# Two-layer hybrid mLSTM and retention trunk on one core: gate bias on VectorE, new product rows begun tile by tile, layer 1's gate transposes a step later

## The chip, the cores and the metric

The kernel runs on one core of a Trainium2 chip. The metric is the device time of one execution in microseconds (us); lower is better. The time before is the median of three runs, 2317.24 us (2315.03 to 2318.58).

## The reference

Everything is in fp32. The sequence has 1024 tokens, the model is 1024 wide, and there are two layers:

```python
c_act = jax.nn.silu(c)
for l in range(DEPTH):
    ada = c_act @ w_ada[l] + b_ada[l]
    shift, scale, gate = jnp.split(ada, 3, axis=-1)
    h = rmsnorm(x, norm_g[l]) * (1.0 + scale[:, None, :]) + shift[:, None, :]
    p = h @ w_in[l]
    ...
    cell = mlstm_chunkwise(mq_c, mk_c, mv, mi + b_igate[l], mf + b_fgate[l])
    y_m = jax.nn.sigmoid(mo) * head_layernorm(cell, gn_m[l], N_HEADS_MLSTM) * jax.nn.silu(mz)
    ret = retention_chunkwise(rq_h, rk_h, rv)
    y_r = head_layernorm(ret, gn_r[l], N_HEADS_RET) * jax.nn.silu(rz)
    y = jnp.concatenate([y_m, y_r], axis=-1) @ w_out[l]
    x = x + gate[:, None, :] * y
return rmsnorm(x, final_g)
```

Four mLSTM heads and four retention heads are 256 wide each. The change touches three places of this: the vector `gate` (the last third of `ada`), the input and forget gates `mi`, `mf` of the mLSTM heads, and the product with `w_out`.

## The kernel before

**Products.** Each fp32 operand is split into a high part in the fp32r format and a low rest, and a product is made of three fp32r matmuls: high by high, low by high and high by low (`mm3`, lines 133 to 136 of the profile's numbering: L134, L135, L136). ScalarE makes the high part (a cast, L600 or L1005), GpSimd (L601) or VectorE (L1013) subtracts it from the operand. The names `wH`, `wL` are the two parts of a weight tile; parts of activations come from the common pool `b`.

**Order.** The order of TensorE's instructions is written out by hand: the program's order is TensorE's order. For the other engines and for the DMA queue (all loads and stores are issued from SyncE's queue, `SP`), a scheduler orders instructions by its own estimate of time, except in the beginning, and on VectorE and ScalarE from the second product row of an output projection on (`ordered`), where the program's order holds. Each engine runs its instructions in order and waits on semaphores.

Side work is written as Python generators that are started with `launch` and resumed by `tick`. `run_units` calls `tick` after each unit of the main work; `yield n` asks to be resumed n ticks later. So the place of side work among TensorE's instructions is counted in units. A unit is usually 12 matmuls of 512 columns.

**The gate vector** (`gate_rows`, L281 to L293) is such a generator. It is launched after head group 5 of each layer. For each half of 512 columns, VectorE sums eight weight tiles, each scaled by the conditioning vector, into `accs[0]` (128 partitions). A matmul with a matrix of ones (L289) sums over the partitions and puts the result on all 128 of them, in a PSUM tile `pt`. A second matmul (L290) adds the bias: its operands are one row of ones and one row `brow`, which a DMA has loaded from `b_ada` (L286). These two have plain fp32 operands. VectorE copies `pt` into `g` (L292). `g` is used in the output projection.

**The mLSTM gates** (`gate_chain`) run once in each layer, as side work beside the first projections. Scans over the sequence give, for each half of it, a tile `T4` with four groups of four rows (the last of them copied at L484). After `yield 3` TensorE transposes the two `T4` (L494, eight transposes of 128 by 128) and VectorE copies the result into `COL` (L495), from which decays and scales are made.

**The output projection** (`out_projection`, `out_units`) makes the product with `w_out` by seven rows of products in the manner of Strassen-Winograd. Each row has eight items (an activation tile `yH`, `yL` and a weight tile) and four PSUM banks, one for each tile of 128 tokens. A class `OutPrep` loads and splits the items, three ahead of the row. An item is 12 matmuls, three on each of the four banks; behind each item stands a `yield`. The last two items of a row are taken tile by tile: three matmuls of the one and three of the other on a bank, then that bank's read-out. Rows with `first=True` begin on new banks: `b1` (pool `pp`, p = 1), `b2` (pool `pa`, p = 5) and `b3` (pool `pp`, p = 7). The pool `pp` has four banks that are given out in turn; before `b1` the projections use them. The last of these is a half of the z projection of head group 7, which ScalarE reads through a tanh (L528) and VectorE through a product (L530, in `z_evac`).

While the first row runs, the attention of head group 7 is still under way as side work: `scores` (products L134 to L136 and L752 into a bank of `pa`; L754 to L757 on VectorE, then the split `sH`, `sL`), `values` and `update`.

Of the kernel before, what the change touches and what calls it, by code (L numbers as in the profile page):

```python
# [15 lines left out]
ALU = mybir.AluOpType  # L16
# [3 lines left out]
P = 128  # L20

D = 1024
# [4 lines left out]
KT = D // P  # L27
# [42 lines left out]
def tile_hybrid_trunk(ctx, tc, x, c, positions, w_ada, b_ada, norm_g, w_in, conv_w, conv_b,  # L70
                      b_igate, b_fgate, gn_m, gn_r, w_out, final_g, consts, out):
    nc = tc.nc
    V, A, G, PE, Q = nc.vector, nc.scalar, nc.gpsimd, nc.tensor, nc.sync
# [17 lines left out]
    def bt(dt=F32, n=512):  # L91
        return big.tile([P, n], dt, tag="b", name=nm("b"))

    def wt(tag, n, bufs, dt=F32):
        return wrk.tile([P, n], dt, tag=tag, bufs=bufs, name=nm(tag))

    def ps_a():
        return pa.tile([P, 512], F32, tag="a", name=nm("pa"))
# [34 lines left out]
    def mm3(o, lt, rt, start, stop, more=False):  # L133
        PE.matmul(o, lt[0], rt[0], start=start, stop=False, skip_group_check=more)  # L134
        PE.matmul(o, lt[0], rt[1], start=False, stop=False, skip_group_check=more)  # L135
        PE.matmul(o, lt[1], rt[0], start=False, stop=stop, skip_group_check=more)  # L136
# [3 lines left out]
    ones = cst.tile([P, P], F32, tag="ones", name="ones")  # L140
# [110 lines left out]
    def ada_rows(l, c0, accs):  # L251
        acc = bt()
        accs.append(acc)
        prev = None
        for k in range(KT + 1):
            raw = None
            if k < KT:
                raw = bt()
                Q.dma_start(raw, w_ada[l, k * P:(k + 1) * P, c0:c0 + 512])
            if k == 1:  # L260
                V.tensor_scalar(acc, prev, cact[:, 0:1], None, ALU.mult)
            elif k > 1:
                V.scalar_tensor_tensor(acc, prev, cact[:, k - 1:k], acc, ALU.mult, ALU.add)
            prev = raw
            yield 2
# [15 lines left out]
    def gate_rows(l, res):  # L281
        for half in range(2):
            accs = []
            yield from ada_rows(l, 2 * D + half * 512, accs)
            brow = wt("th", 512, 5)
            Q.dma_start(brow[0:1, :], b_ada[l, 2 * D + half * 512:2 * D + (half + 1) * 512].unsqueeze(0))  # L286
            yield 2
            pt = ps_a()
            PE.matmul(pt, ones, accs[0], start=True, stop=False)  # L289
            PE.matmul(pt, ones[0:1, :], brow[0:1, :], start=False, stop=True)  # L290
            g = bt()
            V.tensor_copy(g, pt)  # L292
            res.append(g)  # L293

    def norm_scale(xt, sst, act_rows=()):
# [141 lines left out]
    def gate_chain(l, pgs, gt):  # L437
# [21 lines left out]
        for half in range(2):  # L459
# [26 lines left out]
            prev = {"bq": bq[0:4, 511:512], "br": br[0:4, 511:512], "mx": mx[0:4, 511:512]}  # L486
            T4s.append(T4)
            yield 1
        yield 3
        for half in range(2):  # L490
            T4 = T4s[half]
            pt = ps_a()
# [535 lines left out]
    def out_units(prep, banks, first, last, evac, deep=2):  # L1028
        def product(i, piece, tt):
            (yH, yL), w = piece  # L1030
            ts = slice(tt * P, (tt + 1) * P)
            mm3(banks[tt], (yH[:, ts], yL[:, ts]), w, first and i == 0, i == KT - 1, not first)

        for i in range(KT - deep):
            piece = prep.take()
            for tt in range(4):
                product(i, piece, tt)
            yield
        pieces = [prep.take() for _ in range(deep)]
        for tt in range(4):  # L1040
            for i in range(deep):
                product(KT - deep + i, pieces[i], tt)
            evac(tt)
            if deep > 2 or tt % 2:
                yield
# [36 lines left out]
    def out_projection(l, prep, gb, fg, nhT):  # L1082
# [10 lines left out]
        x12, x22, x21 = [None] * 4, [None] * 4, [None] * 4  # L1093
        b1 = [ps_p() for _ in range(4)]
        run_units(out_units(prep, b1, True, False, save(b1, c1, None)))
        for step in (prep.sum_up, prep.sum_up, prep.cast):
            step()
        ordered = tc.manual_schedule(engines={mybir.EngineType.DVE, mybir.EngineType.Activation})
        ordered.__enter__()
        x11 = [residual(l, 0, 0, tt) for tt in range(4)]  # L1100
        run_units(out_units(prep, b1, False, True,
                            lambda tt: out_rows(l, 0, 0, tt, b1[tt], gb, xn[0], ss[0], x11[tt])))
        b2 = [ps_a() for _ in range(4)]
        run_units(out_units(prep, b2, True, False, save(b2, c5, 0)))

        def sum_up(tt):
# [133 lines left out]
    accs = [bt()]  # L1240
# [7 lines left out]
    for l in range(DEPTH):  # L1248
# [14 lines left out]
        if l == 0:  # L1263
# [6 lines left out]
            for step in script.split():  # L1270
# [6 lines left out]
                elif what == "C":  # L1277
                    half, k = seq[n]
                    hT[k][half] = (bt(F32R), bt(F32R))
                    A.copy(hT[k][half][0], hfs[n])  # L1280
                elif what == "U":
                    half, k = seq[n]
# [3 lines left out]
                elif what == "A":  # L1286
                    g, a, b = (int(d) for d in arg)
# [34 lines left out]
        vraw = []  # L1322
        run_units(v0_units(l, load_v0(l) if l else w0, hT, vraw, pgs))
        launch(gate_chain(l, pgs, gt), 1)
        if l == 0:
            wz1 = split_w(rz1[0], P) + split_w(rz1[1], P)
# [7 lines left out]
        for hg in range(8):  # L1334
# [33 lines left out]
            if hg == 5:  # L1368
                launch(gate_rows(l, gb))
# [40 lines left out]
```

## Time and profile before

| | |
|---|---|
| median of three runs | 2317.24 us (2315.03 to 2318.58) |
| the profiled execution: its own time | 2319.17 us |
| its span, first to last instruction | 2317.5 us |
| TensorE busy | 2262.3 us |
| VectorE busy | 1473.7 us |
| ScalarE busy | 955.8 us |
| GpSimd busy | 813.3 us |
| mean granted TensorE clock | 0.993 |

The profile names the engines PE (TensorE's matmuls), PEld (its weight loads), DVE (VectorE), ACT (ScalarE), POOL (GpSimd) and SP (SyncE's DMA queue). A row of a timeline has the start in us from the span's start, the duration in us, the engine, the line of the kernel, the operation, the tiles (written tile, arrow, read tiles), the number of instructions merged in it, and in brackets the engine's idle time before it with what ended it. A row of the view of waits has who waited for whom, the total in us, the number of waits and the longest. A busy PE may still run at half its clock, so starts of successive matmuls tell more than their durations.

### The profile page before, as it was taken

How to read it: one execution, taken by the hardware profiler on the slowest of the kernel's cores; microseconds unless marked ns; L12 is line 12 of the kernel's file. 1: busy time of each engine (PE TensorE's matmuls, PEld its weight loads, DVE VectorE, ACT ScalarE, POOL GpSimd, SP SyncE). 2: the span in 40 equal slices, each digit the busy share in tenths (PEclk: the TensorE clock that was granted, in tenths of full speed). 3: DMA queues.
4: the chain of work that ended last, by engine and by line, in shares of the span. 5: the costliest groups of instructions: out<-in, count | busy, mean ns of one | idle time of the engine just before them, and what ended most of it. 6: DMA issues, size and time to landing. Idle time of an engine off the chain costs nothing. (4 is left out here: it accounts for less than half of the span.)

```text
span 2317.5 us, 35197 instructions
## 1 busy us (share of the span) xinstructions
PE 2262.3 (98%) x12405; PEld 1948.0 (84%) x12405; DVE 1473.7 (64%) x2971; ACT 955.8 (41%) x1868; POOL 813.3 (35%) x777
## 2 busy tenths in 40 slices
PE   5999999999999999999999999999999999999998
PEld 4888888889988988888888888888898888888886
DVE  7386668566575657557865765575655565665677
ACT  5535433444433323345344544444443333333533
POOL 0344343334354434320152433444334443442100
PEclk9999999999999999999999999999999999999999
DMA  7234434454675665676622335454545545645764
GB/s 247 70 77 122 121 82 150 113 167 135 187 214 181 206 203 170 196 272 205 236 74 66 80 103 138 129 175 114 186 128 175 161 139 177 199 128 186 278 197 153
DMA packets 385729, 367.52 MB, mean 159 GB/s; under 512 B 82420, under 2 KB 268540, under 8 KB 385552
## 3 DMA queue, kind: packets, MB, share of 16 engines
q1 hardware_dynamic: 385552, 365.28, 51.9%
q8 instruction: 97, 1.59, 0.3%
q14 instruction: 80, 0.66, 0.1%
HBM read 253.99 MB, written 111.18 MB: 158 GB/s over the span
## 5 line engine op out<-in xcount | busy, mean ns | idle before, releaser
L134 PE MATMUL pp<-b,wH 128*128 128x512 f32 x1792 | 712.1, 397 | 1.3 <-ACT b L1280 1.1
L135 PE MATMUL pp<-b,wH 128*128 128x512 f32 x1792 | 708.8, 396 | 1.4 <-DVE b L1283 1.3
L136 PE MATMUL pp<-b,wL 128*128 128x512 f32 x1792 | 708.8, 396 | 0.6 <-POOL wL L601 0.6
L601 POOL TENSOR_TENSOR wL<-raw,wH 128x512 fp32r<-128x512 f32 x274 | 373.3, 1370 | 446.6 <-ACT wH L600 395.6
L136 PEld LDWEIGHTS pp<-b,wL 128*128 128x128 f32 x1792 | 338.6, 189 | 80.1 <-POOL wL L601 1.1
L134 PEld LDWEIGHTS pp<-b,wH 128*128 128x128 f32 x1792 | 339.1, 189 | 73.1 <-issue 1.5
L135 PEld LDWEIGHTS pp<-b,wH 128*128 128x128 f32 x1792 | 338.9, 189 | 73.2 <-DVE b L1283 2.4
L601 POOL TENSOR_TENSOR b<-acc,b 128x256 fp32r<-128x256 f32 (+1 forms) x208 | 210.5, 1028 | 284.4 <-ACT b L600 268.1
L134 PE MATMUL pp<-wH,b 128*128 128x256 f32 (+1 forms) x1024 | 302.8, 296 | 3.6 <-DVE g L530 3.6
L136 PE MATMUL pp<-wH,b 128*128 128x256 f32 (+1 forms) x1024 | 302.6, 295 | 0.0
L135 PE MATMUL pp<-wL,b 128*128 128x256 f32 (+1 forms) x1024 | 302.1, 295 | 0.0
L600 ACT CAST wH<-raw 128x512 fp32r<-128x512 f32 x274 | 167.2, 616 | 155.3 <-PE pp L135 116.2
L134 PEld LDWEIGHTS pp<-wH,b 128*128 128x128 f32 x1024 | 193.2, 189 | 10.2 <-DVE g L530 4.4
L135 PEld LDWEIGHTS pp<-wL,b 128*128 128x128 f32 x1024 | 193.3, 189 | 5.5
L136 PEld LDWEIGHTS pp<-wH,b 128*128 128x128 f32 x1024 | 193.0, 188 | 5.7
L618 DVE SCALAR_TENSOR_TENSOR acc<-pp,cols,acc 128x511 f32<-128x511 f32 (+2 forms) x192 | 142.2, 741 | 17.6 <-ACT acc L613 15.5
L600 ACT CAST b<-acc 128x256 fp32r<-128x256 f32 (+1 forms) x208 | 94.6, 487 | 137.1 <-DVE acc L695 81.1
L134 PE MATMUL pa<-b,b 128*128 128x256 f32 (+2 forms) x384 | 117.3, 305 | 10.1 <-ACT nd L798 8.1
L601 POOL TENSOR_TENSOR sL<-th,sH 128x384 fp32r<-128x384 f32 x64 | 66.6, 1040 | 153.1 <-ACT sH L600 141.2
L136 PE MATMUL pa<-b,b 128*128 128x256 f32 (+2 forms) x384 | 116.5, 303 | 0.0
L135 PE MATMUL pa<-b,b 128*128 128x256 f32 (+2 forms) x384 | 116.3, 303 | 0.0
L601 POOL TENSOR_TENSOR cL<-cf,cH 128x516 fp32r<-128x516 f32 (+1 forms) x48 | 65.3, 1361 | 92.5 <-ACT cH L600 90.3
(288 smaller groups left out, 3887.1 us busy)
## 6 DMA issues: line engine op xcount, KB each, us to landing
raw<-in_w_in_dram SPq DMA_DIRECT2D x274, 256.0 KB
b<-in_w_ada_dram SPq DMA_DIRECT2D x96, 256.0 KB
tsp<-g SPq DMA_DIRECT2D x96, 256.0 KB
b<-tsp SPq DMA_DIRECT2D x96, 256.0 KB
gdr<-g SPq DMA_DIRECT2D x64, 256.0 KB
ndr<-zt SPq DMA_DIRECT2D x128, 128.0 KB
g<-ndr SPq DMA_DIRECT2D x64, 256.0 KB
g<-gdr SPq DMA_DIRECT2D x64, 256.0 KB
```

Of the source, the lines that this page charges most:

```text
L134: PE.matmul(o, lt[0], rt[0], start=start, stop=False, skip_group_check=more)
L135: PE.matmul(o, lt[0], rt[1], start=False, stop=False, skip_group_check=more)
L136: PE.matmul(o, lt[1], rt[0], start=False, stop=stop, skip_group_check=more)
L600: A.copy(dst[0], src)
L601: eng.tensor_tensor(dst[1], src, f(dst[0]), ALU.subtract)
L618: V.scalar_tensor_tensor(acc[:, d:], pt[:, 0:HALF - d], wcol, acc[:, d:], ALU.mult, ALU.add)
```

## The change

Three edits in one. The bias of the gate vector is loaded into all 128 partitions instead of one, the matmul L290 goes, and VectorE adds the bias in the instruction that copied before. In layer 1 `gate_chain` waits four steps instead of three ahead of its transposes. In a row of products on new banks, the first two items are taken tile by tile, with a `yield` behind each second tile.

```diff
@@ gate_rows @@
             brow = wt("th", 512, 5)
-            Q.dma_start(brow[0:1, :], b_ada[l, 2 * D + half * 512:2 * D + (half + 1) * 512].unsqueeze(0))
+            Q.dma_start(brow, b_ada[l, 2 * D + half * 512:2 * D + (half + 1) * 512].unsqueeze(0).to_broadcast([P, 512]))
             yield 2
             pt = ps_a()
-            PE.matmul(pt, ones, accs[0], start=True, stop=False)
-            PE.matmul(pt, ones[0:1, :], brow[0:1, :], start=False, stop=True)
+            PE.matmul(pt, ones, accs[0], start=True, stop=True)
             g = bt()
-            V.tensor_copy(g, pt)
+            V.tensor_tensor(g, pt, brow, ALU.add)
@@ gate_chain @@
-        yield 3
+        yield 4 if l else 3
@@ out_units @@
-        for i in range(KT - deep):
+        done = 0
+        if first:
+            pieces = [prep.take(), prep.take()]
+            for tt in range(4):
+                for i in range(2):
+                    product(i, pieces[i], tt)
+                if tt % 2:
+                    yield
+            done = 2
+        for i in range(done, KT - deep):
             piece = prep.take()
             for tt in range(4):
                 product(i, piece, tt)
```

In the changed kernel all lines from L287 to L1033 have numbers lower by one, and those behind the inserted block higher by eight.

**The gate vector.** On TensorE, in the middle of a projection of head group 6 in layer 0, before (`pa` is the PSUM tile `pt`, the rows around it are the projection's):

```order
L136 MATMUL pp_1771_9667<-b_121_880,wL_1767_9658 128x512
L289 MATMUL pa_1774_9687<-b_1618_8939,ones_77 128x512
L290 MATMUL pa_1774_9687<-th_1759_9628,ones_77 128x512
L134 MATMUL pp_1771_9667<-b_138_945,wH_1769_9663 128x512
L135 MATMUL pp_1771_9667<-b_139_946,wH_1769_9663 128x512
```

The row L290 is gone in the changed kernel, here and at the three other places; nothing around it moves on TensorE. On VectorE, at the same place, the rows now are (L291 is the addition; the two rows below it read the projection's bank `pp`):

```order
L908 TENSOR_TENSOR g_1773_9685<-g_1773_9685,g_1801_9787 128x512
L291 TENSOR_TENSOR b_1775_9689<-pa_1774_9687,th_1759_9628 128x512
L882 TENSOR_TENSOR g_1803_9793<-g_1802_9792,g_1803_9793 128x512
L692 TENSOR_TENSOR th_1778_9706<-pp_1771_9667,nd_1274_7223 128x512
L693 TENSOR_TENSOR th_1779_9707<-pp_1771_9667,dm_1272_7217 128x512
```

The addition stands where the copy stood, and reads the tile `th` of the bias besides.

**The first row of products.** On TensorE, the beginning of the first product row of layer 0 before, with item 0 on the four banks 2122 to 2125, then a step of the attention's scores:

```order
L134 MATMUL pp_2122_11439<-wH_2079_11260,b_2077_11258 128x512
L135 MATMUL pp_2122_11439<-wL_2080_11261,b_2077_11258 128x512
L136 MATMUL pp_2122_11439<-wH_2079_11260,b_2078_11259 128x512
L134 MATMUL pp_2123_11440<-wH_2079_11260,b_2077_11258 128x512
...
L134 MATMUL pp_2125_11442<-wH_2079_11260,b_2077_11258 128x512
L135 MATMUL pp_2125_11442<-wL_2080_11261,b_2077_11258 128x512
L136 MATMUL pp_2125_11442<-wH_2079_11260,b_2078_11259 128x512
L134 MATMUL pa_2135_11473<-b_1914_10421,b_1990_10767 128x256
```

And in the changed kernel, with items 0 and 1 (`wH_2079` and `wH_2083`) on banks 2122 and 2123, then the scores, then bank 2124:

```order
L134 MATMUL pp_2122_11437<-wH_2079_11258,b_2077_11256 128x512
...
L134 MATMUL pp_2122_11437<-wH_2083_11264,b_2081_11262 128x512
...
L136 MATMUL pp_2123_11438<-wH_2083_11264,b_2082_11263 128x512
L134 MATMUL pa_2145_11491<-b_1914_10420,b_1990_10765 128x256
...
L134 MATMUL pp_2124_11439<-wH_2079_11258,b_2077_11256 128x512
L135 MATMUL pp_2124_11439<-wL_2080_11259,b_2077_11256 128x512
```

The fourth bank comes up behind 18 matmuls of the row and the scores, where it came up behind nine matmuls and ahead of the scores. The scores stand behind 12 matmuls as before.

**The transposes of layer 1.** On TensorE before, in the middle of a half of a projection (bank 14040):

```order
L136 MATMUL pp_14040<-b_13267,wL_13990 128x512
L494 MATMUL pa_14053<-ident,b_13785 128x128 x4
L494 MATMUL pa_14059<-ident,b_13904 128x128 x4
L134 MATMUL pp_14040<-b_13278,wH_13995 128x512
L135 MATMUL pp_14040<-b_13279,wH_13995 128x512
```

And in the changed kernel, at the end of that half:

```order
L134 MATMUL pp_14038<-b_13309,wH_13993 128x512
L135 MATMUL pp_14038<-b_13310,wH_13993 128x512
L136 MATMUL pp_14038<-b_13309,wL_13994 128x512
L493 MATMUL pa_14080<-ident,b_13783 128x128 x4
L493 MATMUL pa_14086<-ident,b_13902 128x128 x4
```

The eight transposes moved behind 12 more matmuls.

## The prediction

> **What bounds the kernel now.** First the page's busy times and the granted clock, in tenths, over 40 slices.
>
> ```profile
> PE 2262.3 (98%) x12405; PEld 1948.0 (84%) x12405; DVE 1473.7 (64%) x2971; ACT 955.8 (41%) x1868; POOL 813.3 (35%) x777
> PEclk9999999999999999999999999999999999999999
> ```
>
> TensorE is busy for 98% of the span at nearly full clock; no other engine comes above 64%. So time goes only where TensorE has fewer instructions, or waits less, or runs less at half clock. Next the waits of TensorE by whom they were for (total us, times, longest):
>
> ```profile
> PE pa L134 <- ACT nd L798: 8.1, 4, 4.2
> PE pp L134 <- DVE g L530: 3.6, 2, 1.8
> PE pa L134 <- ACT n L840: 1.9, 2, 1.7
> PE pa L494 <- DVE b L484: 1.2, 1, 1.2
> ```
>
> Two of these rows are touched by the change: the wait for L530 (a product row's fourth bank, one in each layer) and the wait for L484 (the transposes in layer 1). The other two are not. The third part of the change takes instructions away.
>
> **The gate vector.** TensorE in layer 0, around one of the four places:
>
> ```profile
> 858.16 0.40 PE L135 MATMUL pp<-b,wH 128*128 128x512 f32 x1
> 858.40 0.40 PE L136 MATMUL pp<-b,wL 128*128 128x512 f32 x1
> 858.63 1.02 PE L289 MATMUL pa<-b,ones 128*128 128x512 f32 x2
> 859.58 1.12 PE L290 MATMUL pa<-th,ones 1*128 1x512 f32 x2
> 860.63 0.50 PE L134 MATMUL pp<-b,wH 128*128 128x512 f32 x1
> ```
>
> Starts tell the cost, since matmuls overlap. An fp32r matmul takes 858.40 - 858.16 = 0.24 of the queue, and the plain fp32 product L290, although it has one row to multiply, takes 860.63 - 859.58 = 1.05 (two instructions). Four places make **4.2 us** saved. Nothing hides L290: the work behind it is TensorE's own.
>
> What is added: VectorE reads a second operand where it copied, and a DMA brings 256 KB where it brought 2. The copy and its nearest rows, additions or products with a PSUM operand of the same shape:
>
> ```profile
> 862.94 0.68 DVE L292 COPY b<-pa 128x512 f32<-128x512 f32 x1
> L694 DVE TENSOR_TENSOR th<-pp,dm 128x512 f32<-128x512 f32 x32 | 21.8, 680 | 0.0
> ```
>
> They take 0.68 each, so VectorE has the same work. The load is issued far ahead; the nearest row for its duration is the broadcast of one row for the attention's mask, 128 KB:
>
> ```profile
> 842.39 0.36 SPq L286 DMA_DIRECT2D th<-in_b_ada_dram  x1
> 2039.16 0.32 SPq L286 DMA_DIRECT2D th<-in_b_ada_dram  x1
> 2055.70 1.02 PE L289 MATMUL pa<-b,ones 128*128 128x512 f32 x2
> 1358.00 0.43 SPq L733 DMA_DIRECT2D dm<-mdr  x1
> 1362.41 0.42 POOL L735 TENSOR_SCALAR_AFFINE_SELECT dm<-dm 128x256 f32<-128x256 f32 x1 [6.68 <-DMA dm<-mdr]
> ```
>
> That one took 1362.41 - 1358.00 = 4.4. The bias has 862.94 - 842.39 = 20.6 before VectorE reads it, and at the last place at least 2055.70 - 2039.16 = 16.5. Twice 4.4 for twice the bytes, as an upper bound, is 8.8, still within it. I cost it at nothing; what is hidden is the landing, under the projection's matmuls. If the cover were gone, VectorE would stand at the addition, with the read-outs of the projection's banks behind it, and TensorE behind those.
>
> **The first product row.** Layer 0, all on the engines named:
>
> ```profile
> 1014.84 0.39 PE L135 MATMUL pp<-wL,b 128*128 128x512 f32 x1
> 1015.00 0.60 ACT L528 ACTIVATE th<-pp 128x512 f32<-128x512 f32 x1
> 1015.07 0.40 PE L136 MATMUL pp<-wH,b 128*128 128x512 f32 x1
> 1016.57 0.68 DVE L530 SCALAR_TENSOR_TENSOR g<-th,pp 128x512 f32<-128x512 f32 x1
> 1017.30 0.74 PE L134 MATMUL pp<-wH,b 128*128 128x512 f32 x1 [1.84 <-DVE g L530]
> 1018.69 0.42 PE L134 MATMUL pa<-b,b 128*128 128x256 f32 x1
> 1020.82 0.40 PE L134 MATMUL pp<-wH,b 128*128 128x512 f32 x1
> ```
>
> The fourth bank's first matmul starts 2.23 behind its predecessor instead of 0.23: **2.0** lost. Then three matmuls of 512 columns and ten of 256 take 1020.82 - 1017.30 = 3.52. Layer 1 has the same instructions behind the same wait:
>
> ```profile
> 2142.97 0.40 PE L136 MATMUL pp<-wH,b 128*128 128x512 f32 x1
> 2145.08 0.50 PE L134 MATMUL pp<-wH,b 128*128 128x512 f32 x1 [1.72 <-DVE g L530]
> 2147.05 0.39 PE L134 MATMUL pp<-wH,b 128*128 128x512 f32 x1
> ```
>
> The wait costs 2.11 - 0.23 = **1.9** there, and the 13 matmuls take 1.97. So layer 0 lost **1.55** more after its wait. The windows show why (clock ahead of the last two columns; the third row holds layer 1's same stretch):
>
> ```profile
> 1012.00:1016.00 4.00, 3.47 (x21) 2.71 (x19) 2.33 (x7) 2.54 (x5) 0.82 (x1) 1.00 0.98 327
> 1016.00:1020.00 4.00, 2.69 (x10) 2.41 (x11) 3.09 (x5) 2.21 (x5) 1.28 (x1) 0.67 1.04 374
> 2145.00:2149.00 4.00, 3.92 (x22) 3.43 (x23) 2.89 (x8) 1.73 (x4) 1.78 (x1) 1.00 1.08 382
> ```
>
> The clock fell to 0.67 of full speed in layer 0's stretch and not in layer 1's, after gaps of 2.2 and 2.1. I take the fall as the gap's work, since it is at full clock ahead of it. The Trainium skill (TensorE: Matmul & The Clock Gate, Part 1: The HAM clock gate) says that the array is halved after an idle window of about 3.4 us, whose windows run freely. By an idle time of 3.4 us neither gap would do it, and the 1.55 would have another cause and stay; that the two rows differ at like gaps fits windows whose place in time decides.
>
> In the changed order the fourth bank comes up behind 12 matmuls of 0.23, the scores (ten of 256 columns, 0.12 each) and six more of 0.23: 2.8 + 1.2 + 1.4 = 5.4 behind the row's start, which is 1014.84 - 7 x 0.23 = 1013.2, so at 1018.6. L530 ends at 1017.25, 1.3 earlier. No wait is left if VectorE and ScalarE keep their order there, and the order shows L528 and L530 with the same instructions ahead of them. Item 1 is wanted behind item 0's three matmuls on the first bank, at 1013.2 + 0.7 = 1013.9, where before it was wanted at 1020.82. It is ready:
>
> ```profile
> 997.06 2.31 DVE L1013 TENSOR_TENSOR b<-b,b 128x512 fp32r<-128x512 f32 x2
> ```
>
> These are the last parts of items 0 and 1, done at 999.4, 14 us ahead. The later rows on new banks (b2, b3) cost nothing either way: the view of TensorE's waits lists none from 1047 to 1190 and from 2148 to the end, where they run, and items are split three ahead. What comes next is the attention's values. Before, they stand 24 matmuls behind the scores, now also 24. Their last operand was made in time:
>
> ```profile
> 1023.21 1.02 POOL L601 TENSOR_TENSOR sL<-th,sH 128x384 fp32r<-128x384 f32 x1 [5.03 <-ACT sH L600]
> 1027.36 0.28 PE L136 MATMUL pa<-b,sL 128*128 128x256 f32 x1
> ```
>
> It ends 1024.23 - 1020.82 = 3.4 after the scores, and 24 matmuls are 5.6. The sum of this part is 2.0 + 1.55 + 1.9 = **5.4 us**.
>
> **The transposes of layer 1.**
>
> ```profile
> 1276.41 0.60 PE L494 MATMUL pa<-ident,b 128*128 128x128 f32 x4
> 1277.08 0.99 DVE L484 TENSOR_TENSOR b<-b,b 4x512 f32<-4x512 f32 x1
> 1278.22 0.63 PE L494 MATMUL pa<-ident,b 128*128 128x128 f32 x4 [1.21 <-DVE b L484]
> 1278.60 0.47 PE L134 MATMUL pp<-b,wH 128*128 128x512 f32 x1
> ```
>
> The second four took 0.38. Had the first four taken as much, the second would have begun at 1276.79: 1278.22 - 1276.79 = **1.4** lost. Twelve matmuls later is 2.8 us later, 1279.2, behind L484's end at 1278.07. The wait goes. Behind it, the copies into `COL` come later by less, since VectorE reached them only at 1284.66; the order puts them one instruction later.
>
> ```profile
> 1284.66 0.34 DVE L495 COPY COL<-pa 128x64 f32<-128x64 f32 x2
> 1314.81 0.28 PE L134 MATMUL pa<-b,b 128*128 128x256 f32 x1
> ```
>
> Their users (masks, decays, scaled values) serve an attention whose first scores start 30 us on, and TensorE's waits list none from 1279 to 1361. I cost this at nothing, under those projections; without that cover it would be at most the one step of 2.8 us.
>
> **The sum.** 4.2 + 5.4 + 1.4 = 11.0. From the profiled execution's 2319.17 this gives 2308.2. That execution was 1.9 over the median of the runs, which are what the result will be compared with: 2317.24 - 11.0 = **2306.2 us**.
>
> **The rivals.**
> - *The half clock stays* (the page's rule): all three waits go, but the 1.55 has another cause. 2306.2 + 1.55 = 2307.8. The clock row of 0.67 just behind the gap speaks against it, layer 1's full clock behind a like gap for it. Chance 0.10.
> - *More than the sum*: every later wait meets the clock's windows at another time. The wait of TensorE for L798 in layer 1 (part of the 8.1 above) may lose a slow stretch like the 1.55, or its own 2: some 3.5 more, 2302.7. Chance 0.10.
> - *The wait moves on*: the fourth bank no longer waits, but VectorE and ScalarE, whose order behind L530 is changed, deliver the attention's `sH`, `sL` late. Of 5.4 nothing is kept but 1.4: 2310.2. For it: scores now run before L530 has ended. Against it: 2.2 of slack. Chance 0.10.
> - *New waits eat the gain*: the scheduler moved some instructions on VectorE, ScalarE and GpSimd near the bias and in the output rows. Two or three waits of the size of the one for L840 (1.7), each with a slow stretch (1.55), are 6.5 to 10: 2313 to 2316, no change. Against it: only neighbours swap, and projection weights are split far ahead. Chance 0.08.
> - *The broadcast is late, and the kernel slower*: the bias lands behind VectorE's turn for it. VectorE stands, the projection's banks are not read out, TensorE stands. The price is what the landing exceeds the cover, at four places. It decides beyond 16.5 to 20.6; to be slower by 0.2% (4.6 us) it must eat 11.0 + 4.6 = 15.6, or 3.9 at each place, landings of 20 to 25 us, against 4.4 for half the bytes: about 2322. Chance 0.03.
>
> That an edit does nothing is in the third and fourth: only L290's 4.2 cannot fail.
>
> **How the numbers follow.** The forecast has 0.59, the rivals 0.10, 0.10, 0.10, 0.08 and 0.03. The forecast's own spread is 2304.5 to 2308.5 (the before runs spread by 3.5). The range leaves out no change and slower (0.11) and some of the tails: 2302.5 to 2311.5. A measurement of this kernel can tell about 0.2% (4.6 us) from no change; faster by more is below 2312.6: the forecast and the first three rivals, 0.89, less a little for their tails, 0.87; within 0.2% 0.10; slower 0.03.
>
> **What would show it.** In the profile after: no L290 in TensorE's groups, and starts of L289 and the next matmul 0.95 apart; no wait of TensorE for L530 (then L529) and none for L484; granted clock 1.00 behind the start of the first product row of layer 0; idle time of VectorE ahead of L291 not ended by a DMA. It would be wrong if TensorE's waits grew a new row for `sL`, for the split items (L1012) or for a bank's read-out.

## The result and the profile after

| | before | after |
|---|---|---|
| median of six runs | 2318.18 us (2315.03 to 2323.22) | 2308.82 us (2306.52 to 2311.45) |
| the profiled execution: its own time | 2319.17 us | 2310.99 us |
| its span | 2317.5 us | 2309.3 us |
| mean granted TensorE clock | 0.993 | 0.994 |

The ratio is 0.9959, with a 95% interval of 0.9945 to 0.9972: 9.4 us faster, at least 6.5 and at most 12.8. The forecast was 2306.2. All times here are medians of the fast runs: one execution of experiment 1 (2459.83 us) and one of the kernel before (3178.63), both at a low granted clock (0.848 and 0.655), are left out.

The page's busy times and granted clock, after:

```profile
PE 2255.1 (98%) x12397; PEld 1943.0 (84%) x12397; DVE 1482.1 (64%) x2971; ACT 956.3 (41%) x1868; POOL 813.2 (35%) x777
...
PEclk9999999999999999999999999999999999999999
```

TensorE has eight instructions fewer (four products of two instructions each) and is still the engine that is busy all along. VectorE's work grew by 8.4 us of busy time, at the same share of 64%. The addition of the bias is not what made it grow: experiment 1 below, which has that edit alone, has 1473.8, as before. The view of TensorE's waits, after (total us, times, longest):

```profile
PE pa L134 <- ACT nd L797: 8.9, 4, 3.8
...
PE pa L134 <- ACT n L839: 1.4, 1, 1.4
...
PE pa L493 <- DVE b L483: 0.5, 1, 0.5
```

The row for the fourth bank (L530, now L529), 3.6 us before, is gone altogether. The row for the transposes is still there with 0.5, but it is another place: layer 0, where there was no wait before. The two waits that the change doesn't touch stand at 8.9 and 1.4, where they had 8.1 and 1.9. One row is new, a wait of 0.6 for L806 in layer 0, which reads a PSUM bank; such a row was named as a sign of a wrong forecast. It follows L797's wait there, at 351 us, ahead of every place that the change touches, and experiments 6 and 8 have it with 0.6 too.

TensorE's timeline at the first of the four places of the gate vector, after:

```profile
862.01 0.40 PE L136 MATMUL pp<-b,wL 128*128 128x512 f32 x1
862.25 1.02 PE L289 MATMUL pa<-b,ones 128*128 128x512 f32 x2
862.71 0.80 PE L134 MATMUL pp<-b,wH 128*128 128x512 f32 x1
863.34 0.39 PE L135 MATMUL pp<-b,wH 128*128 128x512 f32 x1
```

From the matmul ahead of L289 to the second one behind, 863.34 - 862.01 = 1.33. Before it began at 858.40, and the second matmul behind L290 stands in this row of before's timeline:

```profile
860.97 0.39 PE L135 MATMUL pp<-b,wH 128*128 128x512 f32 x1
```

That is 2.57, so this place is 1.24 shorter, where 1.05 was forecast. The bias itself is no trouble: the view of L291 (VectorE's addition) after lists what its idle time ended with.

```profile
L291 DVE TENSOR_TENSOR b<-pa,th x4: 683/687/693, 866.8 to 2052.1; 128x512 f32<-128x512 f32 x4
...
its engine sat idle before it (us, times) until:
  PE pa L289: 2.4, 2
```

It takes 0.69 like the copy, and waits for TensorE's product, never for the DMA.

The first product row of layer 0 after, where the scores begin and end, and then where the fourth bank begins (1019.22):

```profile
1016.42 0.39 PE L136 MATMUL pp<-wH,b 128*128 128x512 f32 x1
1016.65 0.28 PE L134 MATMUL pa<-b,b 128*128 128x256 f32 x1
...
1017.82 0.40 PE L134 MATMUL pp<-wH,b 128*128 128x512 f32 x1
...
1018.99 0.40 PE L136 MATMUL pp<-wH,b 128*128 128x512 f32 x1
1019.22 0.39 PE L134 MATMUL pp<-wH,b 128*128 128x512 f32 x1
```

There is no bracket with an idle time. The steps are 0.23 for 512 columns (1019.22 - 1018.99) and 0.12 for 256 columns (ten in 1017.82 - 1016.65), as at full clock before. The windows of the same stretch have the granted clock (ahead of the last two columns) at 1.00 and TensorE busy throughout:

```profile
1013.00:1017.00 4.00, 4.00 (x24) 3.48 (x23) 2.91 (x7) 3.32 (x7) 0.00 (x1) 1.00 0.99 347
1017.00:1021.00 4.00, 4.00 (x23) 3.42 (x22) 2.74 (x7) 2.31 (x5) 2.09 (x2) 1.00 1.07 380
```

The transposes, layer 0 in the first two rows and layer 1 in the third and fourth:

```profile
141.59 0.60 PE L493 MATMUL pa<-ident,b 128*128 128x128 f32 x4
142.73 0.63 PE L493 MATMUL pa<-ident,b 128*128 128x128 f32 x4 [0.54 <-DVE b L483]
...
1275.98 1.03 PE L493 MATMUL pa<-ident,b 128*128 128x128 f32 x8
1276.77 0.48 PE L134 MATMUL pp<-b,wH 128*128 128x512 f32 x1
```

In layer 1 all eight now run in one piece, 0.79 to the next matmul. In layer 0, which the change leaves as it was, the second four wait. Before, TensorE had the eight of layer 0 in one piece (138.99, next matmul 139.78); the extra time after is 143.12 - 141.59 - 0.79 = 0.74.

**Where the profiled pair differs.** Setting each TensorE instruction of after against the same one of before, after is 2.6 us *later* at the end of the start-up (80 us), 3.3 later behind layer 0's transposes, 3.0 earlier behind the first product row of layer 0, 4.6 earlier behind layer 1's transposes, and 8.1 earlier at the end. The first 2.6 have nothing to do with the change: TensorE, VectorE, ScalarE and GpSimd have the same instructions in the same order there, but TensorE runs at half clock in other stretches of the start-up. The last of them is shown by timelines of 18 matmuls behind a wait for VectorE, before first, then after:

```profile
41.98 1.05 PE L248 MATMUL pa<-ones,b 128*128 128x1 f32 x8 [1.94 <-DVE b L243]
...
44.74 0.48 PE L134 MATMUL pp<-b,wH 128*128 128x512 f32 x1
```

```profile
42.22 1.87 PE L248 MATMUL pa<-ones,b 128*128 128x1 f32 x8 [3.95 <-DVE b L243]
...
47.29 0.48 PE L134 MATMUL pp<-b,wH 128*128 128x512 f32 x1
```

The 18 take 2.76 in before and 5.07 in after, where the windows from 42 to 46 us have a granted clock of 0.50 (before, 1.00). So over 2 us of a single pair is scatter, and terms have to be read at their places or from medians. From the end of the start-up on, the pair differs by 2.6 + 8.1 = 10.7.

### The profile page after: what moved, and what is told of

It reads as the page before. It is cut to its first block, busy times and chain, and to the rows that moved or that the text cites. A ratio compares the mean times of both kernels' runs of the same rounds, so it can differ in the third digit from the quotient of the medians.

```text
span 2309.3 us, 35185 instructions
## 1 busy us (share of the span) xinstructions
PE 2255.1 (98%) x12397; PEld 1943.0 (84%) x12397; DVE 1482.1 (64%) x2971; ACT 956.3 (41%) x1868; POOL 813.2 (35%) x777
## 4 chain that ended last, share of the span: by engine, by line
PE 80%; DVE 6%; DMA 6%; issue 3%; POOL 2%; ACT 2%; SPq 1%; POOLq 0%; ACTq 0%; DVEq 0%
PE pp L134 21%; PE pp L136 21%; PE pp L135 21%; PE pa L135 5%; PE pa L134 5%; PE pa L136 5%; PE pa L751 1%; DMA g<-gdr 1%; DMA b<-in_w_ada_dram 1%; POOL wL L600 1%; DMA ndr<-zt 1%; DMA b<-in_x_dram 1%; DVE acc L617 0%; DVE rsd L831 0%; DMA tsp<-g 0%
## 5 line engine op out<-in xcount | busy, mean ns | idle before, releaser
L134 PE MATMUL pa<-b,b 128*128 128x256 f32 (+2 forms) x384 | 117.3, 305 | 10.9 <-ACT nd L797 8.9
```

## The experiments

Each of the three edits was run alone, then the changed kernel with one thing more or less. The times of before beside them are medians of 27 runs (first four kernels, 2317.65 us) and 15 runs (the others, 2315.90 us).

**1. The bias alone.** The edit in `gate_rows` only, as in the first part of the change:

```diff
-            PE.matmul(pt, ones, accs[0], start=True, stop=False)
-            PE.matmul(pt, ones[0:1, :], brow[0:1, :], start=False, stop=True)
+            PE.matmul(pt, ones, accs[0], start=True, stop=True)
...
-            V.tensor_copy(g, pt)
+            V.tensor_tensor(g, pt, brow, ALU.add)
```

> The kernel before with the first edit alone: the bias of the gate vector is added by VectorE, the second plain fp32 product is gone. Theory of the sum (three savings that add up, each at its own place): in the profile the way from the matmul ahead of the gate product to the second one behind it shrinks from 2.57 us to 1.33 us at each of the four places, 5.0 us in all, and the waits for L530 (1.8 in each layer) and L484 (1.2) stay; time 5 us below before, about 2313. Rival (knock-on: the scheduler's new order on VectorE, ScalarE and GpSimd brings or eats time elsewhere): the way at the four places shrinks as said, but TensorE's waits behind them change by over 2 us in all, so the time is off 2313 by as much, beyond the change of the start. Rival (late broadcast): idle time of VectorE ahead of the addition that a DMA ends, and more than 2 us of it. Half clock: the stretch behind the wait for L530 runs at half clock in some layers and at full clock in others.

Measured: 2311.57 us, ratio 0.9971 [0.9959, 0.9983], so 6.1 us less in medians. From the matmul ahead of L289 to the second behind, the four places take 1.32, 1.21, 1.31 and 1.20, against 2.57, 2.46, 2.57 and 2.45 before: 1.25 each, **5.0** in all. VectorE's addition never waits for the DMA. TensorE still waits for the fourth bank, and this run's timeline shows what follows in layer 0:

```profile
1014.04 0.40 PE L136 MATMUL pp<-wH,b 128*128 128x512 f32 x1
1016.24 0.51 PE L134 MATMUL pp<-wH,b 128*128 128x512 f32 x1 [1.80 <-DVE g L529]
...
1018.21 0.40 PE L134 MATMUL pp<-wH,b 128*128 128x512 f32 x1
```

The gap is 2.20, as long as before's 2.23, and the 13 matmuls behind it take 1018.21 - 1016.24 = 1.97 at full steps. Before's 3.52 at this place was not what such a gap has to cost.

**2. The row alone.**

```diff
-        for i in range(KT - deep):
+        done = 0
+        if first:
+            pieces = [prep.take(), prep.take()]
+            for tt in range(4):
+                for i in range(2):
+                    product(i, pieces[i], tt)
+                if tt % 2:
+                    yield
+            done = 2
+        for i in range(done, KT - deep):
```

> The kernel before with the third edit alone: the first two items of a row on new banks tile by tile. Theory of the sum: no wait of TensorE for L530 in either layer, no half clock at the start of the first rows, 3.6 us less in layer 0 (2.0 and the slow stretch of 1.55) and 1.9 in layer 1; time 4 to 5.4 us below before, about 2313; the wait for L484 stays. Rival (the wait moves on): the gap is gone but TensorE waits for the scores' parts sH, sL or another operand of the attention within the next 20 us, and 2 us or less are won. Rival (half clock has another cause): clock below 0.9 in the 4 us behind the start of layer 0's first row though no gap is left.

Measured: 2313.77 us, ratio 0.9981 [0.9968, 0.9993], 3.9 less. TensorE's waits have no row for L530, none for `sL` and none for the row's split items (L1013). At both places the fourth bank starts 0.23 or 0.24 behind its predecessor. The 2.0 and 1.9 are gone, and nothing took their place there. The transposes of layer 1 still wait, in this run's view of waits:

```profile
PE pa L494 <- DVE b L484: 1.1, 1, 1.1
```

**3. The step alone.**

```diff
-        yield 3
+        yield 4 if l else 3
```

> The kernel before with the second edit alone: layer 1's gate transposes a step later. Theory of the sum: the wait for L484 is gone, 1.4 us less at 1276, nothing else; time 1.4 below before, within the spread of the runs. Rival (knock-on): waits of the attention of head group 0 or 1 in layer 1 (for L798) grow by 1 us or more, and nothing is won. Half clock: as in the first run, two more gaps of 2 us at the first rows to see whether a slow stretch follows.

Measured: 2316.76 us, ratio 0.9996 [0.9986, 1.0006]: 0.9 less, which can't be told from none. In the trace the place shrank from 2.50 (from the first transpose to the second matmul behind) to 1.11, so 1.4 went from it. Its timeline shows the fourth bank in layer 0 once more with a gap and no slow stretch behind it:

```profile
1015.71 0.40 PE L136 MATMUL pp<-wH,b 128*128 128x512 f32 x1
1017.45 0.50 PE L134 MATMUL pp<-wH,b 128*128 128x512 f32 x1 [1.34 <-DVE g L530]
1017.79 0.39 PE L135 MATMUL pp<-wL,b 128*128 128x512 f32 x1
```

The three edits alone give 6.1 + 3.9 + 0.9 = 10.9, together 9.4. Within the intervals, some 2 to 3 us to either side of each number, they add up. That none takes from another is shown better by the places: each edit's place is shortened in its own run as it is in after.

**4. Layer 0's transposes a step later too.** The changed kernel with

```diff
-        yield 4 if l else 3
+        yield 4
```

> The changed kernel with the gate transposes a step later in layer 0 too. In the changed kernel's profile they waited 0.5 us for L483 there (0.7 lost); in the profile of before they did not. Theory of the sum: that wait goes, 0.7 us less at 142, the time of the changed kernel less 0 to 0.7, so about 2308.5. Rival: with 2.8 us more the copies into COL come too late for the first scores of layer 0, and TensorE waits there for 1 us or more.

Measured: 2306.59 us, ratio 0.9949 [0.9933, 0.9964]. The timeline has layer 0's eight transposes in one piece:

```profile
140.83 1.03 PE L493 MATMUL pa<-ident,b 128*128 128x128 f32 x8
141.62 0.48 PE L134 MATMUL pp<-b,wH 128*128 128x512 f32 x1
```

The 0.7 is gone from its place, and no wait stands ahead of layer 0's first scores. The medians differ by more, but the intervals overlap widely; a gain of this size can't be read from the times.

**5. The remaining fp32 product in fp32r.** Experiment 4 with L289 made of two fp32r products, the sum being split in two by ScalarE (cast, L603) and GpSimd (subtraction, L604):

```diff
...
-            PE.matmul(pt, ones, accs[0], start=True, stop=True)
+            aH, aL = bt(F32R), bt(F32R)
+            split_to((aH, aL), accs[0])
+            PE.matmul(pt, ones_r, aH, start=True, stop=False)
+            PE.matmul(pt, ones_r, aL, start=False, stop=True)
...
```

> The changed kernel, both layers' gate transposes a step later, and the remaining gate product (L289) in two fp32r matmuls instead of one plain fp32 product (the sum split into a high part by ScalarE and a low one by GpSimd first). Theory (an fp32r matmul holds the queue 0.23 us, the plain fp32 product 0.86): the way from the matmul ahead of the gate product to the second one behind it goes from 1.32 and 1.21 us to about 0.93 at each place, 1.3 us in all; time 1.3 below e4_both, about 2305. Rival: TensorE waits for the low part at these places, 1 us or more each, and the time is above e4_both.

Measured: 2320.31 us, ratio 1.0019 [1.0007, 1.0030], slower than before and some 16 us slower than experiment 4 (1.0019 - 0.9949 of 2316). At the first and third place the parts were ready, and the place takes 0.93 (four steps of 0.23) in place of 1.33. At the second and fourth they were not. Here are this run's waits, then its TensorE and GpSimd timelines at the second place:

```profile
PE pa L293 <- POOL b L604: 6.3, 2, 3.1
...
PE pp L134 <- DVE b L590: 2.1, 1, 2.1
```

```profile
930.10 0.49 PE L292 MATMUL pa<-b,ones 128*128 128x512 f32 x1 [0.57 <-ACT b L603]
933.72 0.50 PE L293 MATMUL pa<-b,ones 128*128 128x512 f32 x1 [3.13 <-POOL b L604]
...
935.51 0.63 PE L134 MATMUL pp<-b,wH 128*128 128x512 f32 x1
```

```profile
932.41 1.26 POOL L604 TENSOR_TENSOR b<-b,b 128x512 fp32r<-128x512 f32 x1
```

The subtraction (932.41 to 933.67) stands in GpSimd's queue behind other splits and ends just ahead of L293's start. Behind it TensorE's matmuls take 0.63 for a while instead of 0.40. To save 0.3 to 0.4 at each place, it lost 3.9 and 4.2 at two of them, with a slow stretch behind each. With these stretches the two places make some 10 of the 17.3 us by which the two profiled executions differ; the rest stands at other waits, such as the one for L590 above, in layer 0 at 897 us, which experiment 4 doesn't have. Whether the edit brought these was not tested.

**6. Only the first row in pairs.** The changed kernel, with the two items tile by tile in the first of the three rows on new banks only:

```diff
-    def out_units(prep, banks, first, last, evac, deep=2):
+    def out_units(prep, banks, first, last, evac, deep=2, pairs=False):
...
-        if first:
+        if pairs:
...
-        run_units(out_units(prep, b1, True, False, save(b1, c1, None)))
+        run_units(out_units(prep, b1, True, False, save(b1, c1, None), pairs=True))
```

> The changed kernel, but only the first of the three rows on new banks is begun tile by tile; the later two are as before. Theory: those two rows waited for nothing, so the time is that of the changed kernel, 2308.8 within the spread, and the profile shows no wait in the rows from 1069 and from 1136 us. Rival (the later rows win something too, an earlier read-out or split): TensorE waits there, or a stage from 1065 to 1190 that is longer than the changed kernel's by 0.5 us or more.

Measured: 2305.19 us, ratio 0.9952 [0.9937, 0.9967], the same as after within the intervals. TensorE's waits have no row for the later product rows, as before the change, and the stretch from 1060 to 1190 us takes as long as in after within 0.1.

**7. A wait that the change leaves.** The largest wait in the middle of the kernel, before and after, is TensorE's for L797. There ScalarE scales a PSUM tile by a column, and TensorE wants the bank again. ScalarE's timeline after shows what L797 stands behind, at the longest wait (3.8, in layer 0) and in layer 1:

```profile
347.82 0.51 ACT L737 ACTIVATE dm<-dm,COL 128x256 f32<-128x256 f32 x1 [3.76 <-POOL dm L734]
...
349.23 0.82 ACT L797 ACTIVATE nd<-pa,wd 128x258 f32<-128x258 f32 x2
...
1358.93 0.72 ACT L883 ACTIVATE g<-g,cols 128x512 f32<-128x512 f32 x1 [1.43 <-DVE g L882]
...
1359.96 0.45 ACT L797 ACTIVATE nd<-pa,wd 128x258 f32<-128x258 f32 x1
```

ScalarE stood waiting for GpSimd's mask (L734) in the one place and for VectorE (L882) in the other, with L797 behind. Both of these stood waiting for a DMA in turn (2.76 at L734, 1.97 at L882). The experiment is number 4 with L797 on VectorE:

```diff
-                        A.activation(nd3[:, tt, 0:W], pi[:, 0:W], AF.Copy, scale=gt["wi"][:, h, j - 1, tt:tt + 1])
+                        V.tensor_scalar(nd3[:, tt, 0:W], pi[:, 0:W], gt["wi"][:, h, j - 1, tt:tt + 1], None, ALU.mult)
```

> e4_both with the scaling of the mLSTM read-out (L797, ScalarE) on VectorE. In all profiles so far TensorE waits 6 to 9 us in three or four places for this line, where ScalarE stands at instructions whose DMA has not landed. Theory (ScalarE's queue is what makes it late): the waits for it shrink from 6 to 3 us or less and the slow stretches behind them go; 3 to 6 us less, about 2302. Rival (VectorE's queue stands behind the same DMAs, L883 and its kind): the waits come back under VectorE's name, and the time is that of e4_both or more.

Measured: 2297.36 us, ratio 0.9919 [0.9902, 0.9936], the fastest version here. By the ratios that is 0.30% or 7 us less than experiment 4; the two intervals just touch. Its waits:

```profile
PE pa L134 <- DVE nd L806: 1.7, 1, 1.7
...
PE pa L134 <- DVE nd L797: 0.5, 1, 0.5
```

6.3 us (experiment 4) became 0.5. Set against experiment 4 instruction by instruction, the profiled execution is 7.9 us shorter, and 5.4 of it stands at the three places where experiment 4 waited for L797 (at 341, 461 and 1353 us). The price is the wait for L806, an instruction behind L797 on VectorE, with 1.7 once: there VectorE itself waits for a DMA (1.05, at L387) between L797 and L806. VectorE's busy time rose to 1500.9 us.

**8. A bias product of 128 rows.** The kernel before, with the bias loaded into all partitions and added by a product with the identity:

```diff
...
-            PE.matmul(pt, ones[0:1, :], brow[0:1, :], start=False, stop=True)
+            PE.matmul(pt, ident, brow, start=False, stop=True)
```

> The kernel before, with the bias product of 128 rows (identity times the bias on all partitions) in place of one row. Theory (a plain fp32 product's cost goes by its columns and not by its rows): the way at the four places stays at 2.57 and 2.46 us, and the time that of before. Rival (rows cost): 0.3 us or more longer at each place.

Measured: one execution, 2312.09 us; what counts is the place in TensorE's timeline:

```profile
857.55 0.40 PE L136 MATMUL pp<-b,wL 128*128 128x512 f32 x1
857.79 1.02 PE L289 MATMUL pa<-b,ones 128*128 128x512 f32 x2
858.64 1.02 PE L290 MATMUL pa<-th,ident 128*128 128x512 f32 x2
859.10 0.80 PE L134 MATMUL pp<-b,wH 128*128 128x512 f32 x1
859.73 0.40 PE L135 MATMUL pp<-b,wH 128*128 128x512 f32 x1
```

2.18, against 2.57 with one row and 1.33 without the product. The product of 128 rows costs 0.85, that of one row 1.24: the smaller one is dearer by 0.39, which neither theory had. The view of weight loads shows the difference, before first, then this run:

```profile
858.40 0.42 PEld L289 LDWEIGHTS pa<-b,ones 128*128 128x128 f32 x2
859.58 0.29 PEld L290 LDWEIGHTS pa<-th,ones 1*128 1x128 f32 x2 [0.76 <-issue]
860.63 0.19 PEld L134 LDWEIGHTS pp<-b,wH 128*128 128x128 f32 x1 [0.76 <-issue]
```

```profile
858.22 0.19 PEld L290 LDWEIGHTS pa<-th,ident 128*128 128x128 f32 x1 [0.24 <-issue]
858.64 0.19 PEld L290 LDWEIGHTS pa<-th,ident 128*128 128x128 f32 x1 [0.24 <-issue]
859.07 0.19 PEld L134 LDWEIGHTS pp<-b,wH 128*128 128x128 f32 x1 [0.24 <-issue]
```

With 128 rows a weight load follows the one before after 0.24 idle. At both changes of the row count it came only after 0.76, and the first matmul on the new weights begins with it instead of behind it.

## Why the prediction was right, and where it was off

- **The gate vector, 4.2.** Right in kind, too small: 5.0 at the four places. The step that was off is the one that took the product's cost as the time from its own start to the next matmul's. That left out that L290 itself started 0.95 behind L289, where in its absence the next matmul starts 0.46 behind (862.71 - 862.25). Against this, the matmul after next came 0.34 behind (860.97 - 860.63) and comes 0.63 behind now. 1.05 + (0.95 - 0.46) - (0.63 - 0.34) = 1.25. For the same reason the forecast mark, starts of L289 and the next matmul 0.95 apart, was wrong: they are 0.46 apart.
- **The first product rows, 5.4.** Both waits went, as forecast, 2.0 and 1.9. The step that failed is the one from "I take the fall as the gap's work" to a full term of the sum: it took a fall seen once for one that such a gap always brings. The kernel before and experiments 1, 3 and 8 have eight such gaps in all, of 1.5 to 2.2 beyond the usual step. One of them, the one that the prediction read, was followed by a slow stretch. The 1.55 was in the profiled execution of before, but by these eight it doesn't belong to the median. The term is **3.9**. Experiment 2's time can't tell that from 5.4: its interval is 1.6 to 7.4 us.
- **The transposes of layer 1, 1.4.** The wait went, in after and in experiment 3, and nothing came late behind it. But its size before is not fixed: where the step is three, the trace shows 1.4 in before and 1.3 in experiment 2, but only 0.3 to 0.4 in experiments 1 and 8. So the edit is worth 0.3 to 1.4.
- **What was not in the sum.** Layer 0's transposes lose 0.7 in after, and nothing in before. This loss comes and goes with no link to an edit: where the step is three, experiments 1, 3, 6 and 8 have it, before and experiment 2 don't, though TensorE, VectorE, ScalarE and GpSimd have the same instructions in the same order up to 135 us in all of them. What makes VectorE late there in some executions stays open; the start-up's scatter was not separated from it.
- **The sum.** 5.0 + 3.9 + 0.3 to 1.4 make 9.2 to 10.3, against 9.4 measured; layer 0's 0.7 is left out, since it may be in executions of either kernel. The forecast of 11.0 was too large by 1.6, from one term too small by 0.8, one too large by 1.55 and one taken at its upper end. That two of these errors went against each other is luck. The time alone doesn't tell the sums apart, since its interval of 6.5 to 12.8 holds all of them; the places do. In the profiled pair, 5.0 + 3.9 + 1.55 + 1.4 - 0.74 = 11.1 read at the places stands against the 10.7 from the end of the start-up on.

The rivals: *the half clock stays* named the right term, 1.55, but not the reason that the runs point to: not another cause, but a gap that slows the clock only sometimes. On the clock gate, the Trainium skill (TensorE: Matmul & The Clock Gate, Part 1: The HAM clock gate) gives an idle window of about 3.4 us and says that windows run freely. That like gaps end differently fits windows that run freely, but no run shows the windows. Gaps well below 3.4 were enough in some runs (2.0 in before), so there the measurement differs from the Trainium skill's figure, and decides. *The wait moves on* and *the broadcast is late* did not happen: no wait for `sL` or a split item in after and experiment 2, and no DMA ahead of L291. *New waits eat the gain* was too strong: 0.7 in layer 0, 0.6 for L806 and 0.8 more for L797, which varies from run to run (6.3 to 8.9 over the nine profiles that leave it on ScalarE). *More than the sum* did not happen.

## What to carry to other kernels

Where one engine is busy for 98%, a change is worth what goes from that engine's own timeline at the place, from the last undisturbed instruction to the next undisturbed one; measured up to the first instruction behind, it misses part. A slow stretch behind a wait in one profile is no term of a sum until a second execution shows it at the same place. And the work that makes TensorE wait may be cheap but queued: moving it out of the queue that stood waiting there (experiment 7) gave some 7 us, while replacing a dear product by cheaper ones that hang on a busy queue (experiment 5) lost more than the change had won.

## What the runs showed of the hardware that was not expected

- A plain fp32 product with one row of weights between products of 128 rows costs 1.24 us, one with 128 rows 0.85. The weight loads show where: at each change of the row count TensorE's weight load stands idle for 0.76 instead of 0.24. That the change of the row count is the reason fits these rows; a one-row product among one-row products was not tried.
- TensorE falls to half clock behind some gaps and not behind others of the same length; what decides is open. Counting each gap of more than 1.0 beyond the usual step, later than 80 us, in the ten profiles: of 14 gaps of 2.7 or more, 12 were followed by a slow stretch that cost 1.3 to 2.6 us. Of 54 gaps of 1.0 to 2.4, 6 were. The two long gaps without one (2.9 and 3.2) were both in experiment 8. Some of the slow stretches began only up to 2 us behind their gap. No slow stretch of five or more matmuls began without such a gap.
